# Stick-breaking diagonal: sigmoids of -z kept in PSUM, masks moved to the products

## The chip, the cores and the metric

One core of one Trainium2 chip runs the whole kernel. The metric is the device time of one execution in microseconds (us). Of the kernel before, three runs are known, with a median of 2426.67 us; a fourth execution was taken with the hardware profiler, and all rows of the trace come from it.

## The reference

One layer over 2048 positions and 1024 channels: an RMS norm, one input projection, three token mixers side by side (a short gated convolution, a convolution of width 31 with a LayerNorm, and stick-breaking attention with 8 heads of 64), an output projection, a squared-ReLU MLP of width 4096, and a final RMS norm. The change concerns the attention alone:

```python
z = jnp.einsum("bhqd,bhkd->bhqk", qb, kb).astype(jnp.float32) * scale
mask = s_idx < t_idx
log_beta = jax.nn.log_sigmoid(z)
log_1m = jnp.where(mask, log_beta - z, 0.0)
suffix = lax.cumsum(log_1m, axis=3, reverse=True) - log_1m
a = jnp.where(mask, jnp.exp(log_beta + suffix), 0.0)
```

With s = sigmoid(z), the weight of a key is s of that key times the product of sigmoid(-z) over all later keys that the mask admits. A masked key counts as 1 in the product and as 0 as a weight.

## The kernel before

The program is recorded by Python generators that are woven together, and a scheduler then sets the order of instructions on every engine by its own model of their durations. At the top, `build` has these stages: `p_start` and `p_half(0)` project the first 1024 positions (to about 250 us); `p_half(1)` projects the others, with the convolution mixer, the splitting of weights (`pre_split`) and the attention of query block 0 (i = 0, 8 heads) woven in; then four calls of `block`, one for each 512 positions, do the output projection and the MLP, and the attention of query blocks 1, 2 and 3 (24 heads in all) is woven into the first three. TensorE (PE) work is in fp32r, each product as three matmuls of split operands (`mm3`, L103, L105, L107).

For each head and query block `a_pass1` makes keys by queries, 128 keys by 512 columns. The diagonal of 512 queries by 512 keys is done in three tiles. The first (L562 on) holds keys of even and odd position against the first 256 queries: two halves of 256 columns, later keys in the left half, earlier keys in the right. The second and the third hold the four residues of keys modulo 4 against the last 256 queries, again two halves each, the latest keys first. Each tile runs so:

- `a_z` (L522, L523) writes z into one PSUM bank with four matmuls of 256 columns. Banks come from the tag `z`, which also gives the transposed products of `a_cross_a` their bank: two banks while query block 0 is worked on, three in the blocks after. PE can write a bank again only when its last reader has finished.
- `a_diag` (L536, L537) makes om = sigmoid(-z) and t = sigmoid(z) on ScalarE (ACT), both 512 columns from PSUM to SBUF; then GpSimd (POOL) masks both in place with an affine select (L541), om with 1 and t with 0.
- Products: POOL multiplies the right half of t by the left half of om (L564, L573), VectorE (DVE) multiplies two halves of om into a running product Rd or R (L566, L575), and in the third tile DVE makes R's right half (L580) and Rd's right half (L582), and POOL multiplies t by R (L581).

Then `a_cross_a` transposes Rd into PSUM on DVE (L616), makes a running product of it (L618 to L635), and its bank is free after L635. For query blocks 1 to 3 the unmasked keys follow (L600 to L604): there the sigmoid of -z already stays in PSUM, and DVE multiplies PSUM by SBUF (L604). `a_pass2` multiplies the weights by the transposed products (L656, L663), splits them (L88, L90) and multiplies by the values (L701, L709, L710). At its end ACT copies the lower half of the output from PSUM into a tile `otmp` (L680), and DVE adds the upper half (L684) into `yc`.

Beside this, in the stage of query block 0, DVE runs the 31 taps of the convolution (L452, one PSUM and one SBUF operand), POOL subtracts for the split of weights (`wpl`, L90), and PE runs the projection (`ps_p`).

Of the kernel before, what the change touches and what calls it, by code (L numbers as in the profile page):

```python
# [15 lines left out]
P = 128  # L16
# [52 lines left out]
class Trunk:  # L69
# [126 lines left out]
    def attention_consts(self, ctx):  # L196
        nc = self.nc
        c = ctx.enter_context(self.tc.tile_pool(name="aconsts", bufs=1))
        self.d1 = c.tile([P, TB], F32, name="d1")
        nc.vector.memset(self.d1, 0.0)  # L200
        nc.vector.memset(self.d1[:, 31:TB:32], 1.0)


    def p_pools(self, ctx):
# [323 lines left out]
        k = keys.rearrange("c (a p b) -> c a p b", a=2, b=J // 2)  # L528
        return [k[:, j % 2, :, j // 2] for j in range(J)]

    def a_diag(self, z, n):

        nc, pool, ab = self.nc, self.at, self.ab
        t = pool.tile([P, TB], F32, name="A0", tag="A0", bufs=ab["A0"])
        om = pool.tile([P, TB], F32, name="om", tag="om", bufs=ab["om"])
        nc.scalar.activation(om, z, AF.Sigmoid, scale=-0.125)  # L536
        nc.scalar.activation(t, z, AF.Sigmoid, scale=0.125)  # L537
        base, cm = ((-1, -2), (256 - 3, -4), (256 - 1, -4))[n]
        for x, fill in ((om, 1.0), (t, 0.0)):
            x = x.rearrange("p (h c) -> p h c", h=2)  # L540
            nc.gpsimd.affine_select(  # L541
                out=x, in_=x, pattern=[[1, 2], [1, 256]], compare_op=ALU.is_gt, fill=fill, base=base, channel_multiplier=cm
            )
        return t, om

    def a_pass1(self, g):
        nc, pool, i = self.nc, self.at, g["i"]
        ab = self.ab
        lo, hi2 = slice(0, 256), slice(256, 512)

        def new(name, bufs, shape=(P, TB), dt=F32):
            return pool.tile(list(shape), dt, name=name, tag=name, bufs=bufs)

        if i:
            g["Kl"] = pool.tile([P, self.kmax], F32R, name="Kl", tag="Kl", bufs=self.ab["Kl"])
            for rows, kq in self.kq_halves(g["h"]):
                to = g["Kl"][rows, : TB * i].rearrange("c (j q) -> c j q", j=2)
                self.load_r(to, kq[:, 0, :, : TB * i // 2])
        A0 = g["A0"] = []

        k2 = [g["Kd"][:, 0:P], g["Kd"][:, 256 : 256 + P]]
        z = self.a_z(g, [(k2[1], lo, lo), (k2[0], lo, hi2)])  # L562
        t, om = self.a_diag(z, 0)
        nc.gpsimd.tensor_tensor(t[:, hi2], t[:, hi2], om[:, lo], op=ALU.mult)  # L564
        Rd = new("R", 2)
        nc.vector.tensor_tensor(Rd[:, lo], om[:, lo], om[:, hi2], op=ALU.mult)  # L566
        A0.append(t)
        yield 1

        k4 = self.every(g["Kd"], 4)  # L570
        z = self.a_z(g, [(k4[3], hi2, lo), (k4[2], hi2, hi2)])
        t, om = self.a_diag(z, 1)
        nc.gpsimd.tensor_tensor(t[:, hi2], t[:, hi2], om[:, lo], op=ALU.mult)  # L573
        R = new("R", 2)
        nc.vector.tensor_tensor(R[:, lo], om[:, lo], om[:, hi2], op=ALU.mult)  # L575
        A0.append(t)
        yield 1
        z = self.a_z(g, [(k4[1], hi2, lo), (k4[0], hi2, hi2)])
        t, om = self.a_diag(z, 2)
# [59 lines left out]
    def a_pass2(self, g):  # L639
        nc, pool, i, h, ab = self.nc, self.at, g["i"], g["h"], self.ab  # L640
        self.v_load(g)
        o = self.ps.tile([P, TB], F32, name="ps_o", tag="o", bufs=1)
        n = 3 + 4 * i
        Vl = None
        late = []
        for k in range(n):
            t = g["A0"][k]
            lo = pool.tile([P, TB], F32R, name="Alo", tag="Alo", bufs=self.ab["Alo"])
            hi = pool.tile([P, TB], F32R, name="Ahi", tag="Ahi", bufs=self.ab["Ahi"])
            if k in (0, 3):  # L650

                Q = self.ps.tile([P, TB], F32, name="ps_q", tag="q", bufs=1)
                nc.vector.transpose(Q, g["ql" if k else "qd"])
            if k < 3:
                qs = Q[:, 0:256] if k == 0 else Q[:, 256:512]
                nc.vector.tensor_tensor(  # L656
                    t.rearrange("p (a c) -> p a c", a=2),
                    t.rearrange("p (a c) -> p a c", a=2),
                    qs.unsqueeze(1).to_broadcast([P, 2, 256]),
                    op=ALU.mult,  # L660
                )
            else:
                nc.vector.tensor_tensor(t, t, Q, op=ALU.mult)  # L663
            self.split(hi, lo, t, "pool")
            v = None
            if k >= 3:
                j = 4 * i - 1 - (k - 3)
                if j % 4 == 3:
                    Vl = pool.tile([P, 4, P], F32R, name="Vl", tag="Vl", bufs=ab["Vl"])
                    vs = self.VS[h][0 : TB * i].rearrange("(p j) c -> p j c", j=4 * i)  # L670
                    self.load_r(Vl, vs[:, j - 3 : j + 1, :])
                v = Vl[:, j % 4, :]
            late.append((k, v, hi, lo))
            if len(late) > ab["late"]:
# [452 lines left out]
```

## Time and profile before

| | before |
|---|---|
| median of three runs | 2426.67 us (2416.28 to 2428.47) |
| the profiled execution's own time | 2415.74 us |
| its span, first to last instruction | 2414.0 us |
| PE matmul busy | 2379.1 us (99%), 11316 matmuls |
| DVE busy | 1534.0 us (64%), 2436 instructions |
| ACT busy | 1043.6 us (43%), 1906 instructions |
| POOL busy | 1128.6 us (47%), 1133 instructions |
| mean granted PE clock | 0.997 of full speed |

In rows of the trace a line number is that of the kernel before, names stand without buffer numbers (`A` is the tile of t, `om` that of sigmoid(-z), `R` both running products), and "idle before <- X" is time in which the engine stood still ahead of the instruction, with what ended it. Matmuls overlap, so PE's busy share is near 100% as long as matmuls follow each other; what tells more is where it is idle, and where the granted clock is below 1.

### The profile page before, as it was taken

Reading aid. Unit: us, or ns where it says so; the run is one execution under the profiler, and the core shown is the slowest. Engines: PE = TensorE matmul, PEld = TensorE weight load, DVE = VectorE, ACT = ScalarE, POOL = GpSimd, SP = SyncE. Lnnn points to the kernel's source line nnn. Section 1 sums busy time; section 2 is a strip of 40 time slices with the busy share of each in tenths; the row PEclk is TensorE's granted clock in tenths of the full one; section 3 lists DMA queues with packets and bytes.
Section 4 is the critical chain, followed back from the end, with each engine's and each line's share of the span. In section 5 each row is a group of like instructions: output and inputs, shape, how many; then the busy total and the mean of one; then the engine's idle time right before and its main releaser. Section 6 shows DMA issues by size and latency. Waiting matters only on the chain.

```text
span 2414.0 us, 32476 instructions
## 1 busy us (share of the span) xinstructions
PE 2379.1 (99%) x11316; PEld 2005.3 (83%) x11316; DVE 1534.0 (64%) x2436; ACT 1043.6 (43%) x1906; POOL 1128.6 (47%) x1133
## 2 busy tenths in 40 slices
PE   8999999999999999999999999999999999999998
PEld 7888877898888888878888888888888888888887
DVE  7966698943898887766676768476667625212114
ACT  5232423342666666544555555355555522121121
POOL 0342477640676666425666665268788720000000
PEclk9999999999999999999999999999999999999999
DMA  7569987789788778687777777866677556655555
GB/s 258 200 234 341 299 269 233 223 265 280 209 225 245 229 206 222 186 300 245 253 234 229 220 242 214 289 200 198 187 202 204 175 183 221 224 187 192 201 183 192
DMA packets 237059, 549.04 MB, mean 227 GB/s; under 512 B 26720, under 2 KB 100448, under 8 KB 218464
## 3 DMA queue, kind: packets, MB, share of 16 engines
q1 hardware_dynamic: 180304, 480.89, 58.9%
q0 software_dynamic: 37504, 56.64, 11.0%
q10 hardware_dynamic: 19088, 9.44, 1.4%
q8 instruction: 89, 1.46, 0.2%
q14 instruction: 74, 0.61, 0.1%
HBM read 390.38 MB, written 148.11 MB: 223 GB/s over the span
## 4 chain that ended last, share of the span: by engine, by line
PE 84%; DMA 6%; DVE 6%; issue 1%; ACT 1%; POOL 1%; SPq 1%; POOLq 0%; DVEq 0%; ACTq 0%
PE ps_y L107 9%; PE ps_y L105 9%; PE ps_y L103 9%; PE ps_u L103 9%; PE ps_u L105 9%; PE ps_u L107 9%; PE ps_p L107 4%; PE ps_p L105 4%; PE ps_p L103 3%; PE ps_z L522 2%; PE ps_z L523 2%; PE ps_x L103 2%; PE ps_x L105 2%; PE ps_x L107 2%; PE ps_o L710 2%; PE ps_o L709 2%
## 5 line engine op out<-in xcount | busy, mean ns | idle before, releaser
L90 POOL TENSOR_TENSOR Alo<-A,Ahi 128x512 fp32r<-128x512 f32 x288 | 385.3, 1347 | 147.0 <-ACT Ahi L88 69.9
L958 DVE TENSOR_TENSOR acc<-acc,ps_y 128x512 f32<-128x512 f32 (+1 forms) x264 | 175.7, 667 | 193.5 <-PE ps_y L107 191.4
L103 PE MATMUL ps_u<-hh,w 128*128 128x512 f32 x1024 | 279.4, 392 | 6.4 <-DMA w<-s_w 6.1
L103 PE MATMUL ps_y<-fh,w 128*128 128x512 f32 (+1 forms) x1056 | 281.2, 384 | 0.0
L105 PE MATMUL ps_y<-fh,w 128*128 128x512 f32 (+1 forms) x1056 | 279.7, 383 | 0.1
L602 POOL TENSOR_TENSOR A<-A,R 128x512 f32<-128x512 f32 x168 | 222.4, 1326 | 121.7 <-ACT A L600 103.3
L107 PE MATMUL ps_y<-fl,w 128*128 128x512 f32 (+1 forms) x1056 | 278.6, 383 | 0.1
L105 PE MATMUL ps_u<-hh,w 128*128 128x512 f32 x1024 | 276.1, 390 | 0.3 <-DVE w L90 0.3
L107 PE MATMUL ps_u<-hl,w 128*128 128x512 f32 x1024 | 275.8, 390 | 0.0
L118 POOL TENSOR_TENSOR rs_y<-rs_v,mhalf 128x4 f32<-128x4 f32 (+1 forms) x13 | 13.2, 1017 | 530.9 <-DVE rs_v L117 486.0
L922 ACT ACTIVATE ps_u<-ps_u 128x512 f32<-128x512 f32 x128 | 74.7, 583 | 399.3 <-PE ps_u L107 399.1
L932 DVE TENSOR_TENSOR fl<-ps_u,fh 128x512 fp32r<-128x512 f32 x128 | 87.7, 685 | 223.3 <-ACT fh L931 222.9
L105 PEld LDWEIGHTS ps_y<-fh,w 128*128 128x128 f32 x1056 | 195.0, 188 | 39.8 <-DMA w<-wraw 0.5
L107 PEld LDWEIGHTS ps_y<-fl,w 128*128 128x128 f32 x1056 | 195.0, 188 | 39.4 <-DVE fl L932 0.6
L88 ACT ACTIVATE Ahi<-A 128x512 fp32r<-128x512 f32 x288 | 176.6, 627 | 117.8 <-PE ps_o L709 51.3
L105 PEld LDWEIGHTS ps_u<-hh,w 128*128 128x128 f32 x1024 | 192.1, 188 | 41.5 <-DVE w L90 0.7
L107 PEld LDWEIGHTS ps_u<-hl,w 128*128 128x128 f32 x1024 | 192.1, 188 | 40.1
L103 PEld LDWEIGHTS ps_y<-fh,w 128*128 128x128 f32 x1056 | 193.6, 188 | 36.8
L103 PEld LDWEIGHTS ps_u<-hh,w 128*128 128x128 f32 x1024 | 186.9, 188 | 42.4 <-DMA w<-s_w 8.1
L604 DVE TENSOR_TENSOR R<-ps_z,R 128x512 f32<-128x512 f32 x168 | 115.7, 689 | 150.6 <-ACT ps_z L601 128.3
L452 DVE SCALAR_TENSOR_TENSOR ps_c<-g,wb,ps_c 128x512 f32<-128x512 f32 x240 | 179.9, 749 | 4.9
L90 DVE TENSOR_TENSOR w<-wraw,w 128x512 fp32r<-128x512 f32 x152 | 150.4, 1008 | 23.7 <-ACT w L88 23.2
(171 smaller groups left out, 4750.7 us busy)
## 6 DMA issues: line engine op xcount, KB each, us to landing
w<-s_w SPq DMA_DIRECT2D x200, 512.0 KB, 3.9
w<-s_w SPq DMA_DIRECT2D x68, 1024.0 KB, 4.8
wraw<-in_w SPq DMA_DIRECT2D x192, 256.0 KB, 5.0
w<-s_w_out SPq DMA_DIRECT2D x64, 512.0 KB, 5.0
s_w<-w SPq DMA_DIRECT2D x32, 1024.0 KB, 5.5
s_w<-w SPq DMA_DIRECT2D x56, 512.0 KB, 4.5
Qd<-KQ SPq DMA_DIRECT2D x64, 256.0 KB, 6.3
xraw<-in_xT SPq DMA_DIRECT2D x48, 256.0 KB, 4.5
```

The source lines that it names most:

```text
L88: nc.scalar.activation(hi, x, AF.Copy)
L90: e.tensor_tensor(lo, x, f(hi), op=ALU.subtract)
L103: self.nc.tensor.matmul(ps, wh, xh, start=start and k == 0, stop=False)
L105: self.nc.tensor.matmul(ps, wl, xh, start=False, stop=False)
L107: self.nc.tensor.matmul(ps, wh, xl, start=False, stop=stop and k == n - 1)
L452: nc.vector.scalar_tensor_tensor(t, g[:, k : k + TB], self.wb[:, c, k : k + 1], t, op0=ALU.mult, op1=ALU.add)
L522: nc.tensor.matmul(z[:, oc], keys, g["qh"][:, qc], start=k == 0, stop=False)
L602: nc.gpsimd.tensor_tensor(t, t, R, op=ALU.mult)
L604: nc.vector.tensor_tensor(Rn, z, R, op=ALU.mult)
L922: nc.scalar.activation(ps, ps, AF.Relu)
L932: nc.vector.tensor_tensor(lo, ps, f(hi), op=ALU.subtract)
L958: nc.vector.tensor_tensor(acc[d][:, cols], acc[d][:, cols], ps, op=ALU.add)
```

## The change

In the first two tiles om is now made for the left half (the later keys) alone, 256 columns; the sigmoid of -z for the right half is written back over z in PSUM and is not masked. DVE multiplies that PSUM half by om into R or Rd, and POOL masks the product in SBUF instead (`a_mask` on R). In the third tile both sigmoids of -z stay in PSUM; the left half's mask is a maximum on DVE with a constant tile `after` (0 where the key is admitted, 1 where not; made once at the start), and the last product, Rd's right half, is masked by POOL. At the end of `a_pass2` ACT copies straight into `yc`, and DVE adds in place.

```diff
+        self.after = c.tile([P, 256], F32, name="after")
+        nc.gpsimd.memset(self.after, 0.0)
+        self.a_mask(self.after, 1, 4, 1.0)
...
+    def a_mask(self, x, j0, J, fill):
+
+        x = x.rearrange("p (h c) -> p h c", c=256)
+        h = x.shape[1]
+        self.nc.gpsimd.affine_select(
+            out=x, in_=x, pattern=[[1, h], [1, 256]], compare_op=ALU.is_gt, fill=fill, base=(256 if J == 4 else 0) - j0, channel_multiplier=-J
+        )
...
-        om = pool.tile([P, TB], F32, name="om", tag="om", bufs=ab["om"])
-        nc.scalar.activation(om, z, AF.Sigmoid, scale=-0.125)
+        om = pool.tile([P, 256], F32, name="om", tag="om", bufs=ab["om"])
+        nc.scalar.activation(om, z[:, 0:256], AF.Sigmoid, scale=-0.125)
         nc.scalar.activation(t, z, AF.Sigmoid, scale=0.125)
...
+        nc.scalar.activation(z[:, 256:512], z[:, 256:512], AF.Sigmoid, scale=-0.125)
+        self.a_mask(om, j, J, 1.0)
+        self.a_mask(t, j, J, 0.0)
...
-        nc.gpsimd.tensor_tensor(t[:, hi2], t[:, hi2], om[:, lo], op=ALU.mult)
         Rd = new("R", 2)
-        nc.vector.tensor_tensor(Rd[:, lo], om[:, lo], om[:, hi2], op=ALU.mult)
+        nc.vector.tensor_tensor(Rd[:, lo], z[:, hi2], om, op=ALU.mult)
+        nc.gpsimd.tensor_tensor(t[:, hi2], t[:, hi2], om, op=ALU.mult)
+        self.a_mask(Rd[:, lo], 0, 2, 1.0)
...
-        nc.vector.tensor_tensor(R[:, lo], om[:, lo], om[:, hi2], op=ALU.mult)
+        nc.vector.tensor_tensor(R[:, lo], z[:, hi2], om, op=ALU.mult)
+        self.a_mask(R[:, lo], 2, 4, 1.0)
...
-        t, om = self.a_diag(z, 2)
-        nc.vector.tensor_tensor(R[:, hi2], om[:, lo], R[:, lo], op=ALU.mult)
+        t = new("A0", ab["A0"])
+        nc.scalar.activation(t, z, AF.Sigmoid, scale=0.125)
+        nc.scalar.activation(z, z, AF.Sigmoid, scale=-0.125)
+        self.a_mask(t, 1, 4, 0.0)
+
+        nc.vector.tensor_tensor(z[:, lo], z[:, lo], self.after, op=ALU.max)
+        nc.vector.tensor_tensor(R[:, hi2], z[:, lo], R[:, lo], op=ALU.mult)
+        nc.vector.tensor_tensor(Rd[:, hi2], z[:, hi2], R[:, hi2], op=ALU.mult)
+        self.a_mask(Rd[:, hi2], 0, 4, 1.0)
         nc.gpsimd.tensor_tensor(t, t, R, op=ALU.mult)
-        nc.vector.tensor_tensor(Rd[:, hi2], om[:, hi2], R[:, hi2], op=ALU.mult)
...
-        tmp = pool.tile([P, TB], F32, name="otmp", tag="om", bufs=ab["om"])[:HD]
-        nc.scalar.activation(tmp, o[HD:P], AF.Copy)
...
+        nc.scalar.activation(y, o[HD:P], AF.Copy)
+        nc.vector.tensor_tensor(y, y, o[0:HD], op=ALU.add)
```

The order of the program moves with it. On DVE, in the second head of query block 0, before, from the product for the third tile to the transpose (`L580` R's right half, `L582` Rd's right half, `L616` the transpose, `L452` taps of the convolution):

```order
L580 TENSOR_TENSOR R<-om,R 128x256
L452 SCALAR_TENSOR_TENSOR ps_c<-g_2_2623,wb,ps_c 128x512
L582 TENSOR_TENSOR R<-om,R 128x256
L452 SCALAR_TENSOR_TENSOR ps_c<-g_2_2623,wb,ps_c 128x512
L616 STREAM_TRANSPOSE ps_t<-R 128x512
```

The same place in the changed program (`L598`, `L599` and `L635` are the same three steps, `L456` and `L454` the taps):

```order
L598 TENSOR_TENSOR R<-ps_z,R 128x256
L456 SCALAR_TENSOR_TENSOR ps_c<-g_2_2636,wb,ps_c 128x512
L599 TENSOR_TENSOR R<-ps_z,R 128x256
L456 SCALAR_TENSOR_TENSOR ps_c<-g_2_2636,wb,ps_c 128x512 x3
L454 TENSOR_SCALAR ps_c<-g_2_2911,wb,b_conv_b 128x512
L456 SCALAR_TENSOR_TENSOR ps_c<-g_2_2911,wb,ps_c 128x512
L346 TENSOR_TENSOR g_3_3030<-ps_p,sig 128x512
L456 SCALAR_TENSOR_TENSOR ps_c<-g_2_2911,wb,ps_c 128x512
L635 STREAM_TRANSPOSE ps_t<-R 128x512
```

Both products now read `ps_z` in place of `om`, and seven instructions instead of one stand between the last product and the transpose, which has to wait for POOL's mask.

On POOL, the same head, before, from the mask of the third tile's om on (`L541` masks, `L573` and `L581` products of t, `L90` and `L337` work of other parts, `L83` loads of values):

```order
L541 AFFINE_SELECT om<-om 128x512
L90 TENSOR_TENSOR wpl<-wraw,wph 128x512
L541 AFFINE_SELECT A_2846<-A_2846 128x512
L573 TENSOR_TENSOR A_2739<-A_2739,om 128x256
L90 TENSOR_TENSOR wpl<-wraw,wph 128x512
L337 TENSOR_TENSOR sig<-sig,R 128x512
L581 TENSOR_TENSOR A_2846<-A_2846,R 128x512
```

The changed program there (`L539` is every mask, `L601` the product of t and R):

```order
L539 AFFINE_SELECT A_2867<-A_2867 128x512
L539 AFFINE_SELECT R<-R 128x256
L90 TENSOR_TENSOR wpl<-wraw,wph 128x512
L83 DMA Vd_3121<-VS 128x256
L90 TENSOR_TENSOR wpl<-wraw,wph 128x512
L90 TENSOR_TENSOR Alo<-A_2659,Ahi 128x512
L341 TENSOR_TENSOR sig<-sig,R 128x512
L601 TENSOR_TENSOR A_2867<-A_2867,R 128x512
L539 AFFINE_SELECT R<-R 128x256
```

The third tile's mask of om is gone from the head of the row; two masks of R, each of which waits for a product on DVE, stand in its place, the last of them behind the product of t and R.

## Rows read from the trace of the kernel before

**Rows 1.** Busy time by stretch: us, then PE, PEld, DVE, ACT, POOL busy, PEclk, DMA.
```profile
300.00:400.00 100.00, 90.14 (x411) 72.82 (x410) 93.34 (x130) 32.89 (x66) 75.47 (x76) 0.97 0.79 261
...
1300.00:1400.00 100.00, 100.00 (x459) 84.40 (x458) 70.92 (x114) 55.32 (x102) 70.52 (x69) 1.00 0.74 233
...
1700.00:1800.00 100.00, 100.00 (x460) 85.11 (x459) 64.41 (x108) 54.52 (x100) 78.99 (x77) 1.00 0.64 193
...
sum 2414.00, PE 2379.07 PEld 2005.35 DVE 1534.03 ACT 1043.58 POOL 1128.55; mean PE 99.13 PEld 83.56 DVE 63.92 ACT 43.48 POOL 47.02
```

**Rows 2.** Waits of PE, whole span: us in total, times, longest.
```profile
PE ps_z L522 <- DVE T L635: 4.8, 3, 3.4
...
PE ps_z L522 <- ACT A L537: 2.7, 1, 2.7
...
PE ps_p L103 <- DVE u L355: 1.0, 1, 1.0
```

**Rows 3.** Timeline from 311 us, second and third head: start, us, engine.
```profile
311.28 4.21 DVE L580 TENSOR_TENSOR R<-om,R 128x256 f32<-128x256 f32 x1
...
313.22 0.28 PE L522 MATMUL ps_z<-Qd,Kd 128*128 128x256 f32 x1
...
313.92 1.29 POOL L337 TENSOR_TENSOR sig<-sig,R 128x512 f32<-128x512 f32 x1
...
316.79 1.98 PE L107 MATMUL ps_p<-xl,wh 128*128 128x512 f32 x8
...
325.42 0.39 PE L522 MATMUL ps_z<-Qd,Kd 128*128 128x256 f32 x1 [3.35 <-DVE T L635]
...
326.75 3.52 PE L107 MATMUL ps_p<-xl,wh 128*128 128x512 f32 x8
...
336.44 0.75 DVE L566 TENSOR_TENSOR R<-om 128x256 f32<-128x256 f32 x1
```

**Rows 4.** Busy time from 320 to 330 us, columns as in rows 1.
```profile
320.00:330.00 10.00, 6.65 (x26) 5.30 (x25) 9.77 (x21) 3.27 (x7) 3.35 (x4) 0.83 0.79 288
```

**Rows 5.** Timeline from 357 us, fourth head.
```profile
357.12 0.28 PE L522 MATMUL ps_z<-Qd,Kd 128*128 128x256 f32 x1
...
366.36 0.39 PE L522 MATMUL ps_z<-Qd,Kd 128*128 128x256 f32 x1 [2.68 <-ACT A L537]
...
366.95 3.06 PE L105 MATMUL ps_p<-xh,wl 128*128 128x512 f32 x8
...
368.57 1.18 DVE L566 TENSOR_TENSOR R<-om 128x256 f32<-128x256 f32 x1
```

**Rows 6.** DVE by line and shape: count, busy us, mean ns, idle before.
```profile
L580 DVE TENSOR_TENSOR R<-om,R 128x256 f32<-128x256 f32 x32 | 37.1, 1158 | 16.1 <-POOL om L541 16.0
...
L582 DVE TENSOR_TENSOR R<-om,R 128x256 f32<-128x256 f32 x32 | 33.0, 1032 | 0.8
...
L575 DVE TENSOR_TENSOR R<-om 128x256 f32<-128x256 f32 x32 | 30.3, 947 | 7.8 <-POOL om L541 7.8
L566 DVE TENSOR_TENSOR R<-om 128x256 f32<-128x256 f32 x32 | 27.0, 844 | 6.7 <-POOL om L541 6.7
...
L958 DVE TENSOR_TENSOR acc<-acc,ps_y 128x256 f32<-128x256 f32 x16 | 6.6, 420 | 4.0 <-PE ps_y L107 3.3
```

**Rows 7.** The tile ps_z: ns min/median/max, first and last start.
```profile
L604 DVE TENSOR_TENSOR R<-ps_z,R x168: 677/691/694, 626.5 to 1918.1; 128x512 f32<-128x512 f32 x168
```

**Rows 8.** POOL by line and shape, columns as in rows 6.
```profile
L541 POOL TENSOR_SCALAR_AFFINE_SELECT om<-om 128x512 f32<-128x512 f32 x96 | 64.7, 674 | 54.6 <-ACT om L536 54.2
...
masks.py:199 POOL TENSOR_SCALAR_AFFINE_SELECT ident<-ident 128x128 f32<-128x128 f32 x1 | 0.3, 293 | 0.1
```

**Rows 9.** ACT by line and shape, columns as in rows 6.
```profile
L536 ACT ACTIVATE om<-ps_z 128x512 f32<-128x512 f32 x96 | 57.0, 594 | 34.5 <-PE ps_z L523 26.3 <-DVE R L566 7.7
...
L813 ACT ACTIVATE sq<-acc 128x256 f32<-128x256 f32 x13 | 5.3, 418 | 14.6 <-DVE acc L958 13.2 <-DVE rs_v L117 1.1 <-DVE ss L814 0.4
```

**Rows 10.** Waits of POOL, columns as in rows 2.
```profile
POOL A L581 <- DVE R L580: 21.9, 22, 4.6
```

More of the change, by code (lines that the diff above doesn't have):

```diff
@@ L529, in every, with a_diag @@
         return [k[:, j % 2, :, j // 2] for j in range(J)]
-    def a_diag(self, z, n):
+    def a_mask(self, x, j0, J, fill):
[4 more added lines that the diff above has]
+        )
+    def a_diag(self, z, j, J):
         nc, pool, ab = self.nc, self.at, self.ab
         t = pool.tile([P, TB], F32, name="A0", tag="A0", bufs=ab["A0"])
-        om = pool.tile([P, TB], F32, name="om", tag="om", bufs=ab["om"])
-        nc.scalar.activation(om, z, AF.Sigmoid, scale=-0.125)
+        om = pool.tile([P, 256], F32, name="om", tag="om", bufs=ab["om"])
+        nc.scalar.activation(om, z[:, 0:256], AF.Sigmoid, scale=-0.125)
         nc.scalar.activation(t, z, AF.Sigmoid, scale=0.125)
[L538 to L543, printed above, removed]
+        nc.scalar.activation(z[:, 256:512], z[:, 256:512], AF.Sigmoid, scale=-0.125)
+        self.a_mask(om, j, J, 1.0)
+        self.a_mask(t, j, J, 0.0)
         return t, om
@@ L562, in a_pass1 @@
         z = self.a_z(g, [(k2[1], lo, lo), (k2[0], lo, hi2)])
-        t, om = self.a_diag(z, 0)
-        nc.gpsimd.tensor_tensor(t[:, hi2], t[:, hi2], om[:, lo], op=ALU.mult)
+        t, om = self.a_diag(z, 1, 2)
         Rd = new("R", 2)
-        nc.vector.tensor_tensor(Rd[:, lo], om[:, lo], om[:, hi2], op=ALU.mult)
+        nc.vector.tensor_tensor(Rd[:, lo], z[:, hi2], om, op=ALU.mult)
+        nc.gpsimd.tensor_tensor(t[:, hi2], t[:, hi2], om, op=ALU.mult)
+        self.a_mask(Rd[:, lo], 0, 2, 1.0)
         A0.append(t)
@@ L571, in a_pass1 @@
         z = self.a_z(g, [(k4[3], hi2, lo), (k4[2], hi2, hi2)])
-        t, om = self.a_diag(z, 1)
-        nc.gpsimd.tensor_tensor(t[:, hi2], t[:, hi2], om[:, lo], op=ALU.mult)
+        t, om = self.a_diag(z, 3, 4)
         R = new("R", 2)
-        nc.vector.tensor_tensor(R[:, lo], om[:, lo], om[:, hi2], op=ALU.mult)
+        nc.vector.tensor_tensor(R[:, lo], z[:, hi2], om, op=ALU.mult)
+        self.a_mask(R[:, lo], 2, 4, 1.0)
+        nc.gpsimd.tensor_tensor(t[:, hi2], t[:, hi2], om, op=ALU.mult)
         A0.append(t)
@@ L678, in a_pass2 @@
             self.a_av(g, o, n, *x)
-        tmp = pool.tile([P, TB], F32, name="otmp", tag="om", bufs=ab["om"])[:HD]
-        nc.scalar.activation(tmp, o[HD:P], AF.Copy)
         if h % 2 == 0:
             self.yc = self.st.tile([P, TB], F32, name="yc", tag="y", bufs=self.ab["yc"])
-        nc.vector.tensor_tensor(self.yc[HD * (h % 2) : HD * (h % 2) + HD], o[0:HD], tmp, op=ALU.add)
+        y = self.yc[HD * (h % 2) : HD * (h % 2) + HD]
+        nc.scalar.activation(y, o[HD:P], AF.Copy)
+        nc.vector.tensor_tensor(y, y, o[0:HD], op=ALU.add)
         if h == H - 1 and i:
```

## The prediction

> **What bounds the kernel now.** I read the busy time by stretch first. PE is busy 2379.07 of 2414 us, and in the stretches of the later query blocks it is busy all the time at a granted clock of 1.00, while DVE, ACT and POOL each have a fifth or more of their time free [rows 1]. There a faster DVE or POOL buys nothing: what counts is whether PE is kept waiting. The stretch from 300 to 400 us is the exception: PE loses 9.86 us, the clock falls to 0.97, and DVE is busy for 93.34 of 100 us [rows 1]. This is the stage of query block 0, where the diagonal and the convolution share DVE. The list of PE's waits then names what PE waited for: the products of `a_cross_a` on DVE (3 times, 4.8 us, the longest 3.4), the sigmoid of a diagonal tile (2.7), a late product of the projection on DVE (1.0) [rows 2]. The timeline shows how the first came about. R's product L580 took 4.21 us, from 311.28 to 315.49, and ended just behind a POOL product that ran from 313.92 to 315.21 [rows 3]; its group's mean is 1158 ns, while an add of the same 256 columns with one PSUM operand takes 420 ns [rows 6]. So a DVE instruction with two SBUF operands is held up while POOL works. DVE was late from there on, and PE stood still for 3.35 us until 325.42 [rows 3]. The stall has a second price: right after it the clock fell (0.83 in the mean of 320 to 330 us [rows 4], so part of it at the lower level of 1.2 GHz), and eight matmuls took 3.52 us, against 1.98 for eight before [rows 3].
>
> **The change part by part, against the profiled execution's 2415.74 us** (10.93 below the median of the runs shown).
>
> *DVE's products.* Removed: four groups of 32, 37.1 + 33.0 + 30.3 + 27.0 = 127.4 us [rows 6]. Added: four of 32 with one PSUM operand, and 32 maxima of z and a constant, 160 of 256 columns. I take 420 ns, the row with one PSUM and one SBUF operand at this size [rows 6], so 67.2 us. The form is not delayed by POOL: L604, a product of PSUM and SBUF, has 677 ns at its shortest and 694 at its longest in 168 instructions [rows 7]. DVE saves 60.2 us, 1.9 us a head. In the later blocks nothing of this lies on the path, since PE is busy there anyway [rows 1]. In the stage of block 0 it is worth what PE's waits cost: 3.35 us, and 3.52 - 1.98 = 1.54 us of lower clock behind it [rows 3]; 2.68 us ahead of the z matmul at 366.36, and 3.06 - 1.98 = 1.08 us behind it [rows 5] (that wait names ACT, but ACT and POOL stood in line behind a DVE that was late); 1.0 us for the product of the projection [rows 2]. Together 9.7 us. The other end is nothing, if DVE stays late for the sake of the taps. I take the whole, because the held-up products were what set DVE back.
>
> How long a product is held up decides the largest term. The row shows one held over several POOL instructions in a row, 4.21 us against 0.42 [rows 3, 6]. The Trainium skill (SBUF — State Buffer, "SBUF: two separate sides") has it that a VectorE instruction with two SBUF inputs and a GpSimd instruction exclude each other, and that the first to start holds the ports for one instruction. By that L580 could have lost no more than one POOL instruction, 1.29 us, and the term for the 3.35 us stall would be nearer 1.3: a gain of 7.6 in place of 9.7. The trace differs in the length, and the trace decides.
>
> *PSUM banks.* This is the cost. Before, the bank of a diagonal tile was free once ACT had read z. Now it is held until DVE has multiplied, and that product waits for POOL's mask of om. Two banks serve block 0, so the third tile's z now waits for the first tile's product. The changed order leaves room: in the third head 51 matmuls stand from the first tile's z to the third's, in the fourth 42. At 459 matmuls in 100 us [rows 1], 0.218 us each, that is 11.1 and 9.2 us. Before, the first tile's product ended 336.44 + 0.75 - 313.22 = 23.97 us after its z in the third head [rows 3], and 368.57 + 1.18 - 357.12 = 12.63 in the fourth [rows 5]. If both were as late again, PE would wait 12.9 + 3.4 = 16.3 us; with DVE on time it would wait nothing. I take 3 us, near the lower end: most of the 23.97 us is the stall itself and the held-up product ahead of it, which go. In the later blocks a third bank is there, and PE never waited for a tile's product.
>
> *POOL's masks.* Before, om's 96 masks of 512 columns took 674 ns each, 64.7 us [rows 8]. Now there are 160 of 256 columns (two of om and three of R a head). Between 293 ns for 128 columns and 674 for 512 [rows 8] a straight line gives 420 ns, so 67.2 us: 2.5 us more in all; between the two rows as bounds it would be 17.8 us less to 43.1 more. The masks of t stay. Three new masks a head wait for DVE; what queues behind them on POOL are splits and products of t. Before, such a wait (t by R for R's product) cost 21.9 us in 32 heads, 0.7 each [rows 10]. Three of these a head, over the 8 heads of a later block, are some 17 us of idle POOL, where POOL is busy for 70.52 to 78.99 of 100 us [rows 1]: the free fifth hides it. The mask of Rd now stands ahead of the transpose, behind the product of t and R. That is about one product and one mask later than before, and DVE's 1.9 us a head pays for it.
>
> *ACT.* om was 96 sigmoids of 512 columns at 594 ns, 57.0 us [rows 9]. Now: 128 of 256 and 32 of 512. At 418 ns for 256 columns [rows 9] this is 53.5 + 19.0 = 72.5 us, 15.5 more in 2414, on an engine busy for 43%. The free time of ACT hides it; if it were gone, it would be half a microsecond a head. The copy of the output's lower half goes to another tile at the same price; in block 0 ACT now waits where DVE did, for that tile's last store, and I set it to nothing. The constant's mask is one instruction at the start. SP's queue issues the same transfers in a slightly other order, which I set to nothing.
>
> **Sum:** -9.7 + 3 = -6.7 us, so 2409.0 for an execution like the profiled one, and 2426.67 - 6.7 = **2420.0 us** for the median.
>
> **Rivals.**
> 1. *The bank becomes the bound (slower).* Place: the third tile's z in block 0. Price: the 16.3 us above, and two more stretches of lower clock at about 1.5 us each, with none of the gain: 2426.67 + 16.3 + 3.1 = 2446 us. It decides from the point where the first tile's product ends later than 11.1 us after its z in the third head, 9.2 in the fourth. For it: 23.97 and 12.63 us before [rows 3, 5], and a POOL at 75.47 of 100 us in that stage [rows 1] with masks queued behind splits. Against it: that lateness had its cause in the products that go. The Trainium skill (Perfetto Trace Analysis, "Optimization Strategy" under "Identifying Performance Opportunities") reads a gap that repeats on the saturated engine as a sign of too little SBUF or PSUM for the next tile; by that rule the change moves the wrong way. The trace of before shows no repeated gap ahead of z, only three or four single ones. Chance 0.14.
> 2. *More of the stage goes than I count (faster).* If all of PE's 9.86 us of 300 to 400 us goes [rows 1], with the 2.6 us of lower clock [rows 3, 5] and the remaining 1.4 us of waits for `a_cross_a` [rows 2], 13.9 us are gained: 2413 us. For it: DVE at 93.34 of 100 us is what nearly all waits there hang on. Against it: POOL's queue stays as long, and some of these waits are chains that no free DVE shortens. Chance 0.24.
> 3. *No change.* The transpose waits for POOL's mask, the next tile waits for the transpose's bank, and the waits that DVE loses come back from POOL; or the products in PSUM are held up as well, and the change does not do what it says. L604's narrow spread [rows 7] speaks against the latter. 2427 us, within 3. Chance 0.22.
>
> **How the numbers follow.** My forecast has 0.40. A measurement of this kernel tells about 0.5% (12 us) from no change. Rival 2 lies at -13.9 us, just past it: faster 0.24. Forecast and rival 3 are both within it: same 0.62. Slower 0.14. The range reaches from somewhat below rival 2, since the runs shown differ by 12 us among themselves, to rival 1: 2404 to 2446 us.
>
> **What would show it.** Right: R's and Rd's products all near 420 ns, none over 1 us; DVE's busy time down by about 60 us, ACT's up by about 15, POOL's about the same; the 3.35 and 2.68 us waits of PE gone, no granted clock below 1 between 320 and 375 us. Wrong: a wait of PE ahead of z that is ended by DVE's product on `ps_z` and repeats from head to head; POOL idle behind masks of R in the blocks; PE below 100 in the stretches after 1100 us; or a time under 2410 us, which would mean that DVE's lateness cost PE more than its listed waits.

## The result, and the profile after

| | before | after |
|---|---|---|
| median of seven runs each, taken side by side | 2417.77 us (2416.12 to 2428.47) | 2404.79 us (2398.47 to 2408.49) |
| ratio of the two, 95% interval | | 0.9932 [0.9916, 0.9947] |
| the profiled execution: its time, its span | 2415.74, 2414.0 us | 2403.54, 2400.8 us |
| mean granted PE clock | 0.997 | 0.998 |

By the medians the change gains 13.0 us, 0.54%; by the ratio of all runs it gains 0.68%, some 16 us, with an interval from 0.53 to 0.84%. The two differ because the seven times of before lie in two groups, four from 2416.12 to 2417.77 us and three from 2426.36 to 2428.47, and their median is the top of the lower group. The two profiled spans differ by 13.2 us. The forecast of 2420.0 us stood on a median of three runs. With four more the median of before came out 8.9 us lower, so 8.9 of the 15.2 us between forecast and result are the base, and 6.3 are the change: 13.0 gained where 6.7 were forecast. Rival 2 (13.9 us) is what happened, as far as these times tell.

The busy time by stretch of the changed kernel shows where; columns as in rows 1 (us, then PE, PEld, DVE, ACT, POOL busy, with counts, PEclk, DMA share, GB/s):

```profile
300.00:400.00 100.00, 99.20 (x479) 82.19 (x478) 88.16 (x145) 37.61 (x78) 86.00 (x94) 1.00 0.88 289
...
1300.00:1400.00 100.00, 100.00 (x459) 84.46 (x459) 69.24 (x117) 56.55 (x108) 68.09 (x72) 1.00 0.76 233
...
1700.00:1800.00 100.00, 100.00 (x452) 84.90 (x451) 59.07 (x107) 54.71 (x103) 78.17 (x78) 1.00 0.62 187
...
sum 2414.00, PE 2373.38 PEld 2004.69 DVE 1484.49 ACT 1047.80 POOL 1123.36; mean PE 98.89 PEld 83.53 DVE 61.85 ACT 43.66 POOL 46.81
```

PE's 9.86 us of idle time between 300 and 400 us [rows 1] have become 0.80, and the clock is at 1.00. In the later blocks PE was full and is full. The count in brackets says the same in work done: 479 matmuls in place of 411. For the whole stage, and as the yardstick of all that follows, here is the same view for 270 to 400 us, of before:

```profile
270.00:400.00 130.00, 120.00 (x553) 97.65 (x552) 118.21 (x167) 45.41 (x91) 95.77 (x98) 0.97 0.82 274
```

and of the changed kernel, with the ten microseconds in which the clock of before fell to 0.83 [rows 4]:

```profile
270.00:400.00 130.00, 129.20 (x619) 107.34 (x618) 112.91 (x187) 51.31 (x107) 106.94 (x119) 1.00 0.90 300
...
320.00:330.00 10.00, 10.00 (x50) 8.38 (x49) 8.52 (x19) 3.40 (x8) 6.82 (x8) 1.00 0.96 334
```

66 more matmuls are done between 270 and 400 us. At 129.20 / 619 = 0.209 us each that is a lead of 13.8 us, about the whole gain. (Both kernels had done nearly the same before: 1376 and 1379 by 270 us.) The waits of PE in the changed kernel:

```profile
PE ps_u L103 <- DMA w<-s_w: 7.2, 5, 2.0
PE ps_p L315 <- ACT wh L88: 6.3, 1, 6.3
...
PE ps_z L526 <- DVE T L654: 1.6, 2, 1.2
PE ps_R L134 <- POOL rs_y L118: 1.1, 1, 1.1
```

Of [rows 2] the sigmoid of a diagonal tile (2.7) and the product of the projection (1.0) are gone, and the wait for `a_cross_a` fell from 4.8 to 1.6. No wait of PE for a product on `ps_z` has come. DVE by line and shape (count, busy us, mean ns, idle before):

```profile
L90 DVE TENSOR_TENSOR w<-wraw,w 128x512 fp32r<-128x512 f32 x152 | 157.7, 1056 | 22.6 <-ACT w L88 21.9 <-DMA wraw<-in_w 0.3
...
L635 DVE STREAM_TRANSPOSE ps_t<-R 128x512 f32<-128x512 f32 x56 | 40.5, 724 | 22.1 <-POOL R L539 21.5
...
L597 DVE TENSOR_TENSOR ps_z<-ps_z,after 128x256 f32<-128x256 f32 x32 | 13.7, 428 | 22.9 <-ACT ps_z L594 22.9
L599 DVE TENSOR_TENSOR R<-ps_z,R 128x256 f32<-128x256 f32 x32 | 13.5, 423 | 0.8
L598 DVE TENSOR_TENSOR R<-ps_z,R 128x256 f32<-128x256 f32 x32 | 13.5, 420 | 4.9 <-POOL R L539 4.2
L576 DVE TENSOR_TENSOR R<-ps_z,om 128x256 f32<-128x256 f32 x32 | 13.3, 417 | 6.0 <-POOL om L539 3.2 <-ACT ps_z L552 2.7
L586 DVE TENSOR_TENSOR R<-ps_z,om 128x256 f32<-128x256 f32 x32 | 13.3, 417 | 7.6 <-POOL om L539 4.7 <-ACT ps_z L552 2.9
```

The products of [rows 6], 844 to 1158 ns in the mean, now take 417 to 428, together 67.3 us for 127.4.

### The profile page after: what moved, and what is told of

It is laid out like the page before. It is cut to its first block, busy times and chain, and to the rows that moved or that the text cites. A ratio compares the mean times of both kernels' runs of the same rounds, so it can differ in the third digit from the quotient of the medians.

```text
span 2400.8 us, 32750 instructions
## 1 busy us (share of the span) xinstructions
PE 2373.4 (99%) x11316; PEld 2004.7 (84%) x11316; DVE 1484.5 (62%) x2468; ACT 1047.8 (44%) x1970; POOL 1123.4 (47%) x1199
## 4 chain that ended last, share of the span: by engine, by line
PE 90%; DMA 5%; DVE 2%; POOL 1%; issue 1%; ACT 0%; SPq 0%; POOLq 0%; DVEq 0%; ACTq 0%
PE ps_y L103 10%; PE ps_y L105 10%; PE ps_y L107 10%; PE ps_u L103 9%; PE ps_u L105 9%; PE ps_u L107 9%; PE ps_p L103 4%; PE ps_p L105 4%; PE ps_p L107 4%; PE ps_z L526 3%; PE ps_z L527 3%; PE ps_x L103 2%; PE ps_x L105 2%; PE ps_x L107 2%; DMA w<-s_w 2%; PE ps_o L720 2%
## 5 line engine op out<-in xcount | busy, mean ns | idle before, releaser
L90 POOL TENSOR_TENSOR Alo<-A,Ahi 128x512 fp32r<-128x512 f32 x288 | 385.1, 1346 | 162.8 <-ACT Ahi L88 88.1
L118 POOL TENSOR_TENSOR rs_y<-rs_v,mhalf 128x4 f32<-128x4 f32 (+1 forms) x13 | 13.2, 1016 | 520.8 <-DVE rs_v L117 476.2
L456 DVE SCALAR_TENSOR_TENSOR ps_c<-g,wb,ps_c 128x512 f32<-128x512 f32 x240 | 180.0, 750 | 4.6
L90 DVE TENSOR_TENSOR w<-wraw,w 128x512 fp32r<-128x512 f32 x152 | 157.7, 1056 | 22.6 <-ACT w L88 21.9
```

The source lines that it names most:

```text
L90: e.tensor_tensor(lo, x, f(hi), op=ALU.subtract)
L456: nc.vector.scalar_tensor_tensor(t, g[:, k : k + TB], self.wb[:, c, k : k + 1], t, op0=ALU.mult, op1=ALU.add)
```

## The experiments

Each batch ran on one chip beside the kernel before, and is compared with its own runs of it. The table has the median, the ratio to before with its 95% interval, and the matmuls done from 270 to 400 us (before 553, after 619; every kernel has 11316 in all).

| run | median us | ratio | matmuls, 270 to 400 us |
|---|---|---|---|
| sbuf_products | 2429.32 | 1.0030 [1.0016, 1.0043] | 537 |
| first_two_tiles | 2425.15 | 1.0011 [0.9999, 1.0024] | 548 |
| third_tile | 2416.94 | 0.9978 [0.9968, 0.9988] | 591 |
| dve_load | 2418.67 | 0.9985 [0.9972, 0.9997] | 609 |
| hold_banks | 2420.80 | 0.9998 [0.9988, 1.0007] | 568 |
| copy_to_otmp | 2405.49 | 0.9930 [0.9917, 0.9942] | 620 |
| no_wpl_on_pool | 2407.79 | 0.9941 [0.9927, 0.9955] | 612 |
| load_off_chain | 2412.43 | 0.9959 [0.9947, 0.9972] | 596 |
| block0_only | 2404.48 | 0.9931 [0.9911, 0.9951] | 617 |
| later_blocks_only | 2421.15 | 0.9990 [0.9974, 1.0005] | 560 |
| after_no_wpl | 2406.11 | 0.9934 [0.9909, 0.9959] | 618 |
| planned_load_block0 | 2417.02 | 0.9987 [0.9974, 1.0000] | 617 |

### Does the operand in PSUM matter? (sbuf_products)

The changed kernel with sigmoid(-z) in SBUF tiles again; masks and the order of the code as in the changed kernel (the third tile's sigmoid in two pieces of 256 columns):

```diff
-        nc.scalar.activation(z[:, 256:512], z[:, 256:512], AF.Sigmoid, scale=-0.125)
+        om2 = pool.tile([P, 256], F32, name="om2", tag="om2", bufs=1)
+        nc.scalar.activation(om2, z[:, 256:512], AF.Sigmoid, scale=-0.125)
...
-        nc.vector.tensor_tensor(Rd[:, lo], z[:, hi2], om, op=ALU.mult)
+        nc.vector.tensor_tensor(Rd[:, lo], om2, om, op=ALU.mult)
...
-        nc.vector.tensor_tensor(z[:, lo], z[:, lo], self.after, op=ALU.max)
+        nc.vector.tensor_tensor(om, om, self.after, op=ALU.max)
```

> The changed kernel, with masks and products where the change puts them, but the sigmoids of -z for the earlier keys (and both of the third tile) written to SBUF tiles in place of PSUM, so that DVE's products have two SBUF operands again; in the third tile ACT writes two pieces of 256. Theory (a product with two SBUF operands is held up while POOL works, and this is what made DVE late in the stage of query block 0): the five products and maxima rise from 0.42 us to a mean of 0.8 us or more, with single ones over 2 us, PE loses 8 us or more again between 270 and 400 us, and the time is 0.4% or more above that of the changed kernel: 2414 to 2422 us. Rival (the gain came from the moved masks and the other order of the program, not from the operand): the products are slow, yet PE keeps its pace, 2400 to 2410 us.

It measured 1.0030: the whole gain is gone, and more. Two of its five groups on DVE:

```profile
L601 DVE TENSOR_TENSOR om<-om,after 128x256 f32<-128x256 f32 x32 | 44.5, 1389 | 12.8 <-ACT om L597 12.7
...
L577 DVE TENSOR_TENSOR R<-om,om 128x256 f32<-128x256 f32 x32 | 25.7, 802 | 4.7 <-POOL om L539 4.7
```

The operations and sizes are the same, the operands are elsewhere, and 428 and 417 ns become 1389 and 802. The gain hangs on this. Two more things differ and may add to the loss: `om2` has one buffer, and the scheduler set another order. The length of the products is the operands' doing: with one of them in PSUM none took more than 433 ns in the changed kernel. Not all of the loss is the stage's: from 600 to 1000 us this kernel does 1818 matmuls, for 1851 before.

### Which tiles, and which block? (first_two_tiles, third_tile, block0_only, later_blocks_only)

first_two_tiles keeps the third tile as before (all four runs here copy straight into `yc`, as the change does):

```diff
+        om = pool.tile([P, TB], F32, name="om3", tag="om3", bufs=1)
+        nc.scalar.activation(om, z, AF.Sigmoid, scale=-0.125)
...
-        nc.vector.tensor_tensor(z[:, lo], z[:, lo], self.after, op=ALU.max)
-        nc.vector.tensor_tensor(R[:, hi2], z[:, lo], R[:, lo], op=ALU.mult)
+        nc.vector.tensor_tensor(R[:, hi2], om[:, lo], R[:, lo], op=ALU.mult)
```

> The change in the first two tiles alone: the third tile as before, both sigmoids of -z in SBUF, masked by POOL, two products with two SBUF operands. Of the 92.6 us above 0.42 us that the four products cost before... here the two of the third tile stay, 70.1 of 127.4 us busy. Theory (held-up products): L580's kind are held up again, with 2 us and more for single ones in the stage of block 0; 40 to 60% of the gain stays, 2408 to 2414 us. Rival (the gain hangs on one chain, that of the third tile): nothing of the gain stays, 2414 us or more. Rival (order): 2400 to 2407 us.

third_tile is the kernel before with the third tile of the change:

```diff
+        nc.scalar.activation(z, z, AF.Sigmoid, scale=-0.125)
...
+        nc.vector.tensor_tensor(z[:, lo], z[:, lo], self.after, op=ALU.max)
+        nc.vector.tensor_tensor(R[:, hi2], z[:, lo], R[:, lo], op=ALU.mult)
```

> The change in the third tile alone: the first two tiles as before (om of 512 columns in SBUF, masked by POOL, products with two SBUF operands, 57.3 of the 127.4 us). Three small constant tiles are moved to another pool to make room. Theory (held-up products): the two large holders go, half or more of the gain stays, 2406 to 2412 us. Rival (the masks moved in the first two tiles make the gain): 2413 to 2420 us.

The first two tiles alone gain nothing, the third alone 0.22%, a third of the whole (in the stage 38 of the 66 matmuls). The expectation's 92.6 us is a slip: 127.4 us less 128 products at 0.42 us leave 73.6. With the first two alone the products that stayed in SBUF got longer than they had been, 1303 and 1184 ns for 1158 and 1032 [rows 6]:

```profile
L594 DVE TENSOR_TENSOR R<-om,R 128x256 f32<-128x256 f32 x32 | 41.7, 1303 | 22.8 <-POOL om L535 17.7 <-POOL R L535 5.1
L595 DVE TENSOR_TENSOR R<-om,R 128x256 f32<-128x256 f32 x32 | 37.9, 1184 | 0.8
```

From 270 to 400 us alone, these two took 15.9 + 7.7 = 23.6 us in 8 products; all four groups of before had taken 24.1 us in 16 (below). This half of the change moved the hold-up to the next products with two operands in SBUF. The parts don't add up: 0 and a third make one.

block0_only and later_blocks_only make the choice by query block:

```diff
+        fresh = i == 0
...
+        if fresh:
+            nc.vector.tensor_tensor(Rd[:, lo], z[:, hi2], om, op=ALU.mult)
...
+        else:
+            nc.gpsimd.tensor_tensor(t[:, hi2], t[:, hi2], om[:, lo], op=ALU.mult)
+            nc.vector.tensor_tensor(Rd[:, lo], om[:, lo], om[:, hi2], op=ALU.mult)
```

> The change for the 8 heads of query block 0 alone; the 24 later heads run as before (sigmoids of -z in SBUF, products with two SBUF operands). Three small constants moved to another pool to make room. Theory (the whole gain is made in the stage of query block 0, where PE waited for DVE): 2400 to 2409 us, PE within 6 us of its own pace between 270 and 400 us, though three quarters of the products are held up as before. Rival (the gain is the sum of 32 heads): a quarter of it, 2413 to 2418 us.

> The change for the 24 heads of query blocks 1 to 3 alone, the first 8 as before. Theory (PE is never late there): no gain, 2414 to 2422 us, with the stalls of before between 270 and 400 us. Rival (sum over heads): three quarters of the gain, 2404 to 2410 us.

The eight heads of block 0 alone give 0.9931, all that the change gives; the other 24 give 0.9990, within the noise. The busy time of block0_only from 270 to 400 us:

```profile
270.00:400.00 130.00, 128.85 (x617) 106.93 (x617) 111.04 (x186) 51.92 (x108) 105.67 (x117) 1.00 0.90 301
```

and of later_blocks_only:

```profile
270.00:400.00 130.00, 120.21 (x560) 99.15 (x559) 120.47 (x170) 45.84 (x90) 99.29 (x103) 0.97 0.83 277
```

### Is it POOL that holds the products up? (no_wpl_on_pool, after_no_wpl)

Part of POOL's work in that stage, the 24 subtractions for `wpl`, is taken away instead, from the kernel before, and then from the changed one (the low parts of those weights are left out, the high parts are stored twice):

```diff
-            lo = self.mx.tile([P, TB], F32R, name="wpl", tag="Rs", bufs=4)
-            self.split(hi, lo, raw, "pool")
-            for n, x in enumerate((hi, lo)):
+            self.nc.scalar.activation(hi, raw, AF.Copy)
+            for n, x in enumerate((hi, hi)):
```

> The kernel before, without POOL's 24 subtractions of the pre-split (1.32 us each, 31.6 us): the high parts of those weights are stored twice in place of high and low parts, so the output is not the reference's. The diagonal's products keep two SBUF operands. Theory (a product is held up while POOL works): the same products are faster between 270 and 400 us (mean under 1.0 us against 1.5), and most of the 13.7 us of the stage is gained with not one operand moved to PSUM, 2403 to 2411 us. Rival (two SBUF operands are slow by themselves, or the gain came from less DVE work): products as slow as before, 2414 to 2424 us.

> The changed kernel without POOL's 24 subtractions of the pre-split (high parts of those weights stored twice, so the output is not the reference's). In the kernel before, leaving them out gained about as much as the change. Theory (both take away the same hold-ups): together they gain no more than 3 us over the changed kernel, 2399 to 2406 us. Rival (POOL's queue was a limit of its own, and the two gains add): 2388 to 2395 us.

About the same gain (0.9941) without touching an operand, and none on top of the change (0.9934). The first is the stronger: in the changed kernel PE is busy for 129.20 of the stage's 130 us, so whatever a second remedy took away, nothing was left there to gain. DVE's products from 270 to 400 us in the kernel before:

```profile
L580 DVE TENSOR_TENSOR R<-om,R 128x256 f32<-128x256 f32 x4 | 9.9, 2483 | 3.2 <-POOL om L541 3.2
...
L575 DVE TENSOR_TENSOR R<-om 128x256 f32<-128x256 f32 x4 | 5.6, 1410 | 1.8 <-POOL om L541 1.8
L582 DVE TENSOR_TENSOR R<-om,R 128x256 f32<-128x256 f32 x4 | 4.9, 1225 | 0.0
...
L566 DVE TENSOR_TENSOR R<-om 128x256 f32<-128x256 f32 x4 | 3.7, 922 | 0.6 <-POOL om L541 0.5
```

and without the subtractions on POOL:

```profile
L575 DVE TENSOR_TENSOR R<-om 128x256 f32<-128x256 f32 x5 | 6.4, 1288 | 1.8 <-POOL om L541 1.8
...
L566 DVE TENSOR_TENSOR R<-om 128x256 f32<-128x256 f32 x5 | 4.1, 816 | 1.6 <-POOL om L541 1.6
L582 DVE TENSOR_TENSOR R<-om,R 128x256 f32<-128x256 f32 x4 | 3.6, 900 | 0.0
L580 DVE TENSOR_TENSOR R<-om,R 128x256 f32<-128x256 f32 x4 | 3.4, 846 | 0.0
```

POOL's busy time there falls from 95.77 to 78.74 us, and the products from 1.5 us in the mean (24.1 us in 16) to 0.97 (17.5 in 18). Only some of the hold-ups went: L580 fell from 2483 to 846 ns, but L575 only from 1410 to 1288, and PE did 612 matmuls all the same. This run also shortens POOL's queue, so alone it would not tell a held-up DVE from a late POOL. In the changed kernel POOL is busier than ever (106.94 us) and PE full: a busy POOL does no harm by itself. That both changes act through the same hold-ups is the reading that fits both.

### Do the banks cost anything? (hold_banks)

The kernel before, with a product of four columns on DVE that reads the bank behind each tile's last product, so that it is held as long as in the change:

```diff
+    def hold(self, z, r):
+        self.nc.vector.tensor_tensor(z[:, 0:4], z[:, 0:4], r[:, 0:4], op=ALU.mult)
...
+        self.hold(z, Rd[:, lo])
```

> The kernel before, and behind the last product of each diagonal tile a DVE product of 4 columns that reads the tile's bank, so that the bank is held as long as in the changed kernel, while the products stay held up: the cost of the banks alone. As predicted, with the lateness of before: 12.9 + 3.4 us of waits ahead of z in the third and fourth head at most, 2425 to 2440 us. Theory now (the scheduler knows of the bank and places z later, and 50 matmuls of room are enough): no more than 3 us, 2415 to 2424 us.

0.9998. Waits for the held bank do appear, in the waits of PE of this kernel:

```profile
PE ps_z L522 <- DVE ps_z L547: 4.0, 3, 2.7
```

but they stand where others stood, and the stage does 568 matmuls for 553. Net of what the other order gives, the banks' price is at most 0.1%; in the changed kernel no such wait came at all.

### Does the copy into yc matter? (copy_to_otmp)

```diff
+        tmp = pool.tile([P, TB], F32, name="otmp", tag="otmp", bufs=1)[:HD]
+        nc.scalar.activation(tmp, o[HD:P], AF.Copy)
...
-        nc.scalar.activation(y, o[HD:P], AF.Copy)
-        nc.vector.tensor_tensor(y, y, o[0:HD], op=ALU.add)
+        nc.vector.tensor_tensor(self.yc[HD * (h % 2) : HD * (h % 2) + HD], o[0:HD], tmp, op=ALU.add)
```

> The changed kernel with the copy at the end of a_pass2 as before (through otmp, in a tile of its own; three small constants moved to another pool to make room). Theory: this part is worth nothing, 2400 to 2409 us. Rival (the copy ahead of yc takes work off ACT's or DVE's queue or frees om): 2411 us or more.

0.9930, the change's own ratio: it doesn't.

### DVE's time, or the delay of the chain? (dve_load, load_off_chain, planned_load_block0)

These give the changed kernel's DVE time back: some 55 us in dve_load, 61 in load_off_chain, 35 in planned_load_block0. dve_load takes the maximum five times, on the chain of the diagonal:

```diff
-        nc.vector.tensor_tensor(z[:, lo], z[:, lo], self.after, op=ALU.max)
+        for _ in range(5):
+            nc.vector.tensor_tensor(z[:, lo], z[:, lo], self.after, op=ALU.max)
```

> The changed kernel with the maximum of the third tile done five times instead of once (the result is the same): 128 more DVE instructions of 0.43 us with one PSUM operand, 55 us more busy time, so that DVE is as busy as before the change (about 1540 us), with no product held up by POOL. Theory (being held up at the wrong moment counts): PE's stalls stay away, 2400 to 2410 us. Rival (DVE's sum of busy time in the stage counts): DVE is late again and PE loses 6 us or more between 270 and 400 us, 2411 to 2420 us.

load_off_chain fills a part of Rd that is written later anyway, seven times a head; planned_load_block0 sixteen times in the heads of block 0 alone (`range(0 if i else 16)`):

```diff
         self.a_mask(Rd[:, lo], 0, 2, 1.0)
+        for _ in range(7):
+            nc.vector.memset(Rd[:, hi2], 1.0)
```

> The changed kernel with seven fills of the not yet written half of Rd per head (256 columns each, overwritten later, nothing waits for them but DVE's own queue): about 55 us more DVE busy time, as in dve_load, but off the chain from z to the transpose and without holding a PSUM bank. In dve_load the stage of query block 0 kept its pace (5.3 us over PE's own pace against 3.7 in the changed kernel and 17.4 before), and the time was lost between 600 and 900 us, in waits for the transpose's bank. Theory (what counts is the chain of a head, from its z to the release of the transpose's bank, and a held-up product is a delay in that chain): the time stays at 2400 to 2409 us. Rival (DVE's sum of work in the first MLP block is the limit, where it is busy for 85 of 100 us): 2413 to 2420 us, lost between 600 and 900 us.

> The changed kernel with 16 fills of 272 ns in each of the 8 heads of query block 0 (4.35 us a head: what the products between 270 and 400 us lost by being held up, 24.1 us in 4 heads against 6.7 at 0.42 each, is 4.35 a head as well), behind which nothing waits but DVE's own queue. The scheduler knows of these and orders the rest around them. Rival (lost DVE time is what costs): the stage is as slow as before, 15 us or more over PE's own pace, 2413 to 2420 us. Theory (a delay that the order of the program was not made for, inside the chain of a head, is what costs): less than half of it comes back, 2403 to 2411 us.

All three lose a part of the gain or nearly all of it, none where it was expected. By their totals dve_load (2418.67 us) and planned_load_block0 (2417.02) came out where the rivals put them, and load_off_chain (2412.43) between the two. dve_load nearly keeps pace in the stage (609 for 619) and loses behind it, from 600 to 1000 us, where PE waits for T (`a_cross_a`) six times, 8.6 us. That stretch of dve_load, and then of the changed kernel:

```profile
600.00:1000.00 400.00, 387.12 (x1788) 321.53 (x1787) 332.72 (x563) 239.98 (x462) 257.30 (x292) 1.00 0.76 216
```

```profile
600.00:1000.00 400.00, 398.39 (x1856) 333.45 (x1855) 327.28 (x533) 250.34 (x480) 264.10 (x296) 1.00 0.75 217
```

load_off_chain loses part in the stage (596), with one wait of PE there, 4.0 us for ACT's `Ahi`. planned_load_block0 has the stage at full pace and is behind ahead of it; its busy time for the two stretches:

```profile
0.00:270.00 270.00, 259.62 (x1335) 221.99 (x1336) 195.12 (x306) 94.64 (x176) 76.26 (x70) 0.99 0.74 252
270.00:400.00 130.00, 128.85 (x617) 106.83 (x616) 116.58 (x243) 48.13 (x102) 97.23 (x109) 1.00 0.91 301
```

By 270 us it is 44 matmuls behind the changed kernel's 1379, about 9 us, though only 16 of its fills, 4.4 us, run there; PE waits there for DVE's `vt` (2.7 us) and `g` (1.5), which it does not in the changed kernel, and why is open. So its total says little of the stage. The stage itself says more. DVE's fills and taps in it, from 270 to 400 us:

```profile
L456 DVE SCALAR_TENSOR_TENSOR ps_c<-g,wb,ps_c 128x512 f32<-128x512 f32 x60 | 43.4, 723 | 0.5
...
L580 DVE MEMSET R<- 128x256 f32 x64 | 17.4, 272 | 2.7 <-POOL A L603 0.3
```

64 fills put back 17.4 us, as much as the hold-ups of before had taken (below). DVE is busy for 116.58 us there, nearly the 118.21 of before, and yet PE loses two matmuls, not 66; no_wpl_on_pool, with DVE busy for 119.21 us, did 612. DVE's busy time is thus not the whole cause. A possible reading is that the scheduler plans a fill, and puts other work elsewhere (60 taps here for 67 in the changed kernel), while a hold-up is in no plan and sets back everything that was placed behind it. But the fills of load_off_chain are planned as well, and there 28 of them in the stage, 7.6 us, go with 23 matmuls lost. No run varied this alone, so it stays open.

## Why the prediction was half right

**Place and cause: right.** The gain is made in the stage of query block 0 and by nothing else (block0_only, later_blocks_only), by the end of the hold-ups of two-operand products (sbuf_products, no_wpl_on_pool). How a hold-up makes PE late, by the time that DVE loses or by the delay in a head's chain, is open. The named stalls went, with the lower clock behind them: 0.83 from 320 to 330 us [rows 4] is 1.00. The sign that the prediction had named for a gain beyond the listed waits, a time under 2410 us, came too, but by luck in part: on the median that the forecast stood on, 13.0 us less would have been 2413.7. Nor does it tell much that 2404.79 us lies just within 2404 to 2446: the lower end was set by the spread of the runs and by no mechanism.

**DVE's 67.2 us: right,** 67.3 measured, and none over 433 ns. Of the 60.1 us saved, 49.5 show in the engine's total, mainly since `w` (L90), two operands in SBUF too, rose from 1008 to 1056 ns, 7.3 us in 152. PE stayed full in the later blocks all the same.

**The term of the stage, -9.7: mis-sized,** the first step that failed. I added up three of PE's waits, 7.0 us, and the lower clock behind two of them, 2.6. The stage gave 13.8 us, 9.2 of them idle time of PE and 4.6 a faster pace. Three more waits of before lie in it (270 to 400 us), which I left out:

```profile
PE ps_R L134 <- POOL rs_y L118: 1.7, 1, 1.7
...
PE ps_z L522 <- DMA yraw<-Y: 0.7, 1, 0.7
PE ps_mean L461 <- ACT cb L456: 0.4, 1, 0.4
```

All that is left there in the changed kernel is 0.8 us for `cb`. I had most of this in hand as rival 2: all of PE's 9.86 us of idle time and 2.6 us of lower clock; the other waits for `a_cross_a`, which it adds, lie outside the stage. I also spread DVE's saving evenly, 1.9 us a head. In the stage itself the four groups took 9.9 + 5.6 + 4.9 + 3.7 = 24.1 us in 16 products, 6.0 a head; sixteen at 420 ns are 6.7, so some 17 us of DVE came free in 130 us in which it was busy for 118. The hold-ups were longest in the one stage where DVE was short (L580: 2483 ns there, 1158 in the mean).

**The banks, +3: failed,** the second step. hold_banks puts them at nothing, and so rival 1 falls. With both terms put right the sum is -13.8 us. The timeline of the changed kernel shows how near it was (start, us, engine; third head, then fourth):

```profile
320.53 0.28 PE L526 MATMUL ps_z<-Qd,Kd 128*128 128x256 f32 x1
...
325.76 0.42 DVE L576 TENSOR_TENSOR R<-ps_z,om 128x256 f32<-128x256 f32 x1 [1.23 <-POOL om L539]
...
331.30 0.28 PE L526 MATMUL ps_z<-Qd,Kd 128*128 128x256 f32 x1
...
352.17 0.28 PE L526 MATMUL ps_z<-Qd,Kd 128*128 128x256 f32 x1
...
361.31 0.42 DVE L576 TENSOR_TENSOR R<-ps_z,om 128x256 f32<-128x256 f32 x1
...
362.30 0.68 PE L526 MATMUL ps_z<-Qd,Kd 128*128 128x256 f32 x1
```

The first tile's product ended 5.65 us after its z in the third head, and the third tile's z came at 10.8, near the 11.1 that I had counted from the order. In the fourth it ended at 9.56, with the next z at 10.1: half a microsecond to spare, though past the 9.2 us from which rival 1 would have had PE wait. So 23.97 and 12.63 us of before [rows 3, 5] became 5.65 and 9.56. In the later blocks PE had waited once before for a product on `ps_z` (0.4 us, L604), where I had said never. With DVE loaded the wait does come in block 0, if small: in planned_load_block0 PE waits twice for L576, 1.1 us. The Trainium skill's reading of repeated gaps (Perfetto Trace Analysis, "Optimization Strategy") found nothing to bear on: ahead of z the changed kernel has two waits, 1.6 us in all, and hold_banks measured 0.9998.

**POOL and ACT: hidden, as said; sizes a little off.** The 160 masks of 256 columns took 43.4 + 29.9 = 73.3 us, 67.2 predicted. POOL by line and shape:

```profile
L539 POOL TENSOR_SCALAR_AFFINE_SELECT R<-R 128x256 f32<-128x256 f32 x96 | 43.4, 454 | 19.3 <-DVE R L576 15.2 <-DVE R L586 2.5 <-DVE R L599 1.4
...
L539 POOL TENSOR_SCALAR_AFFINE_SELECT om<-om 128x256 f32<-128x256 f32 x64 | 29.9, 467 | 46.8 <-ACT om L550 46.6
```

The new masks of R cost POOL 19.3 us of idle time in all, 0.2 each for the 0.7 taken. The transpose, whose wait for POOL's mask I had set against DVE's 1.9 us a head, waits 21.5 us in all, 0.7 a head. PE's waits for T fell nevertheless: at the place shown ahead, the scheduler put seven other instructions in between. Sigmoids of 256 columns took 378 and 380 ns, not 418, and ACT's total rose by 4.2 us, not 15.5:

```profile
L550 ACT ACTIVATE om<-ps_z 128x256 f32<-128x256 f32 x64 | 24.2, 378 | 29.9 <-PE ps_z L527 29.7
...
L552 ACT ACTIVATE ps_z<-ps_z 128x256 f32<-128x256 f32 x64 | 23.8, 380 | 0.8
```

The copy into `yc` at nothing was right (copy_to_otmp).

## What to carry to other kernels

When a stage has one engine that is short of time, price a change by that stage's own rows: the idle time of PE there with the clock behind it is the ceiling, and a change that takes away the cause can get nearly all of it, not a few of the listed waits alone. An operand left in PSUM is worth more than the operation's duration says, if it makes a two-operand product independent of POOL; but where only some of such products move, the hold-up can pass to the next: two of the three tiles gained nothing here. In the later blocks, on full PE, the same edit was worth nothing.

## What the hardware did that I had not expected

- A held-up product waits through several POOL instructions. The longest L582 of the kernel before took 4.73 us, the L580 of [rows 3] 4.21, against 1.29 us for one POOL product and 0.42 without the hold-up. Between the start of that L580 at 311.28 and its end at 315.49 us POOL ran these, and behind them L337 [rows 3], with no gap:

```profile
311.38 0.61 POOL L541 TENSOR_SCALAR_AFFINE_SELECT A<-A 128x512 f32<-128x512 f32 x1
...
311.96 0.73 POOL L573 TENSOR_TENSOR A<-A,om 128x256 f32<-128x256 f32 x1
...
312.66 1.29 POOL L90 TENSOR_TENSOR wpl<-wraw,wph 128x512 fp32r<-128x512 f32 x1
```

The Trainium skill (SBUF — State Buffer, "SBUF: two separate sides") has the exclusion, and that whoever starts first keeps the ports for its instruction; this case's trace agrees on the exclusion, and shows waits longer than one instruction. Products with one operand in PSUM were free of it, at most 433 ns beside a POOL at 106.94 of 130 us.

- Not only instructions with two tiles in SBUF were long: `ca<-u,wa` (L358 of the kernel before), which multiplies one tile in SBUF by a column of weights, took 444 ns at its shortest and 1537 at its longest.
- Where hold-ups were taken from some instructions, others got longer (1303 for 1158 ns in first_two_tiles, 1056 for 1008 in `w`).
- Of 13.8 us in the stage, 9.2 are PE's idle time (120.00 to 129.20 us busy); the rest is pace (217 ns a matmul before, 209 after, the mix of shapes in it too), with the clock at 0.97 and 1.00. A stall cost a second time, in the lower clock behind it (0.83 [rows 4]).
